# Weights split by casting and accumulating DMAs instead of by VectorE

## The chip, the cores and the metric

The kernel runs on one core of a Trainium2 chip, as one launch. The metric is device time in microseconds. A core has TensorE (PE, the matrix engine), VectorE (DVE), ScalarE (ACT), GpSimd (POOL) and SyncE (SP). Each engine works through its own queue strictly in order and waits on semaphores for the others. Transfers between DRAM and the on-chip memory are issued from an engine's queue: in the kernel before, nearly all from SP, and nine constants from POOL. They are carried by 16 shared DMA engines.

## The reference, cut to what matters

One inference step of a two-layer backbone on 640 tokens (512 latent, 128 context) of width 2048, all in float32:

```
layer 0: h = rmsnorm(x)*(1+scale)+shift          # scale, shift, gate: silu(c) @ mod_w[l] + mod_b[l]
         q,k,v,g_attn,hy_in,g_hy = split(h @ w_in)
         att = windowed attention (16 heads, per-head sink, rotary)
         hy  = order-2 long convolution of hy_in (FFT, implicit filters)
         x  += gate * (concat(att*silu(g_attn), hy*silu(g_hy)) @ w_out)
layer 1: h = rmsnorm(x)*(1+scale)+shift
         xb, gate = split(h @ c_w_in);  xc = depthwise_conv(xb)
         r, i = sigmoid(xc @ wa), sigmoid(xc @ wx)   # per head, two directions
         y  = linear recurrences over time in both directions
         x  += gate1 * ((y*silu(gate)) @ c_w_out)
outputs: rmsnorm(x), the new key and value cache, the final recurrent states
```

Nearly all the arithmetic is in five products of the 640 tokens with large weights: `w_in` (2048 x 6400), `w_out`, `c_w_in` (2048 x 4096), the gate matrices and `c_w_out`.

## The kernel before, in words

**Two-part products.** TensorE is given operands of type float32r, to which a value is rounded with fewer mantissa bits. To keep float32 precision each operand is split: a first part `h` (the value rounded to float32r) and a rest `l` (value minus first part). A product is the sum of three: first x first, first x rest, rest x first. For the weights these parts are the tiles `wh` and `wl`, for the tokens `h`/`l` (`mh`/`ml` or `md`, `xhl` in later stages).

**Halves.** Weights come as chunks of 128 output columns, each in two halves of 8 x 128 rows: one half is a tile of [128, 8, 128] float32, 512 KB. Each half is used by 48 matmuls (8 row blocks x 2 token halves x 3 products, lines 823 to 835), so that a half is the unit in which PE asks for weights. There are 241 of them.

**Stream (lines 453 to 519)** prepares halves in a fixed order. `load` issues the transfer of a half into a `raw` tile on the SP queue; `advance` makes `wh` by an ACT copy with a cast; `finish` makes `wl` by a DVE subtraction `raw - wh`, and then loads up to `RAWS` = 3 halves further. `keep_ahead`, called before each row block of a product, calls `advance` while fewer than two halves beyond the one in use are split; `take` hands a half to the product. The pool holds three tiles each of `raw`, `wh` and `wl`.

**Order.** The program is written out by a planner at build time: `Clock` estimates when each instruction would be done, `Order` is a heap of tasks (evictions, attention steps, filters, scans) that are let in between the matmuls when their estimated time has come. The engines then run their queues in exactly that order. `side_mods` (line 661) is one such task: it computes the later modulation vectors from `mod_w`, in tiles `macc` and `mprod`, and decides by the planner's estimate whether a piece goes to DVE alone or to ACT and POOL.

**Stages.** Start (norms, filter spectra, first modulations and the gate chunks), to 365 us of the profile; attention with the first chunks of `w_in`, to 690; the long convolution with the rest of `w_in`, to 1187; `w_out` with the first residual, to 1440; the recurrent layer (`c_w_in` and gate matrices), to 2050; `c_w_out` with the final norm, to the end. The weight stream runs through all of them without a break.

Of the kernel before, what the change touches and what calls it, by code (L numbers as in the profile page):

```python
# [10 lines left out]
F32 = mybir.dt.float32  # L11
F32R = mybir.dt.float32r
AF = mybir.ActivationFunctionType
ALU = mybir.AluOpType
# [7 lines left out]
GL = 644  # L22
P0 = 514
TWO_PI = 2.0 * np.pi
RAWS = 3
SPARE = 0.6


# [146 lines left out]
class Clock:  # L175
# [17 lines left out]
    def __init__(self):  # L193
        self.t = {"PE": 0.0, "V": 0.0, "S": 0.0, "G": 0.0, "Q": 0.0, "DMA": 0.0}
        self.table, self.last = None, 0.0
        self.writes, self.reads, self.start = {}, {}, {}
        self.held = {"V": [], "G": []}
# [255 lines left out]
class Stream:  # L453


    def __init__(self, engines, clock, pool, ahead=2):
        self.V, self.S, self.G, self.Q = engines
        self.pooled = False
        self.clock, self.pool, self.ahead = clock, pool, ahead
        self.src, self.raw, self.parts, self.left = [], {}, {}, {}  # L460
        self.loaded = self.split = self.taken = 0
# [4 lines left out]
    def load(self, n):  # L466
        while self.loaded < min(n, len(self.src)):
            i = self.loaded
            t = self.pool.tile([128, 8, 128], F32, tag="raw", name="raw")
            self.Q.dma_start(out=t, in_=self.src[i])  # L470
            self.raw[i] = t
            self.loaded += 1

    def advance(self):

        i = self.split
        if i >= len(self.src):
            return
        self.load(i + 1)
        raw = self.raw.pop(i)  # L480
        wh = self.pool.tile([128, 8, 128], F32R, tag="wh", name="wh")
        wl = self.pool.tile([128, 8, 128], F32R, tag="wl", name="wl")
        self.S.copy(wh, raw)
        self.parts[i] = (wh, wl)
        self.split += 1
        self.left[i] = raw
        Ring.order.spawn(self.rest(i))
# [6 lines left out]
    def finish(self, i):  # L494

        if i not in self.left:
            return
        raw, (wh, wl) = self.left.pop(i), self.parts[i]
        (self.G if self.pooled and i % 2 else self.V).tensor_sub(wl, raw, wh.bitcast(F32))
        self.load(i + 1 + RAWS)  # L500

    def take(self, od):
        i = self.taken
# [19 lines left out]
@with_exitstack  # L523
def tile_kernel(ctx: ExitStack, tc: tile.TileContext, A: dict, O: dict):
    with tc.manual_schedule():
        _kernel(ctx, tc, A, O)


def _kernel(ctx, tc, A, O):
# [4 lines left out]
    od = Ring.order = Order(clock)  # L534

    def pool_of(stack, name, bufs=1, **kw):
        return Pool(stack.enter_context(tc.tile_pool(name=name, bufs=bufs, **kw)), clock, bufs)
# [3 lines left out]
    wpool = pool_of(ctx, "wpool", bufs=3)  # L541
# [4 lines left out]
    r_acc = Bank(pacc, [128, 512], F32, "acc", 3)  # L546
    r_m = Ring(pmisc, [128, 512], F32, "m", 1)
    ws = Stream((V, S, G, Q), clock, wpool)
# [112 lines left out]
    def side_mods(groups, raws, accs, prods, ring):  # L661
        todo = [(l, g, k) for l, g in groups for k in range(16)]
        raw, n = {}, 0
        for j, (l, g, k) in enumerate(todo):
# [17 lines left out]
            for v in range(2):  # L682
                c, a = csil[:, k, v:v + 1], acc[v]
                while True:
                    if clock.t["V"] + IDLE[0] <= od.time and not left[v] and clock.ready([a], [a], "V") <= od.time:
                        if k == 0:
# [270 lines left out]
    with ExitStack() as st:  # L957
# [9 lines left out]
        msb = sp.tile([128, 512], F32, tag=f"ef{EF}", name="msb", bufs=1)  # L967
        csil32 = sp.tile([128, 16, 32], F32, tag=f"ef{EF + 1}", name="csil32", bufs=1)
# [16 lines left out]
        for i in range(2):  # L985
            G.dma_start(out=fil[i], in_=A["fil"][i])
        mods = Mods(
            [(0, 4 + g // 2 if g % 2 == 0 else g // 2) for g in range(8)],
            [(wpool, "raw", 3), (wpool, "wh", 3), (wpool, "wl", 3)], r_acc, csil32, msb,
        )  # L990
        AHEAD = 7
        mods.load(2)
# [627 lines left out]
            V.tensor_scalar(fr[:, :, i, :], yv[:, :, i, :], sc, None, op0=ALU.mult)  # L1620

    IDLE = [99]
    mods = ctx.enter_context(ExitStack())
    mp = pool_of(mods, "mods", bufs=1)
    r_raw = Ring(mp, [128, 512], F32, "mraw", 2)
# [261 lines left out]
    first_out = []  # L1887
    IDLE[0] = 0.5
    with ExitStack() as st:
# [332 lines left out]


    def out_project(op, layer, src, parts, first, keep, finish, xout, sqa, last=None):

        r_x = Ring(op, [128, T], F32, "xr", 3 if last else 2)
# [9 lines left out]
        def out(i, x, o):  # L2236
# [10 lines left out]
            def then():  # L2247
                r_x.free(x)
                if keep is not None:
                    Q.dma_start(out=keep[i], in_=o[:, 0:T])  # L2250
                if i == 0:
                    S.activation(sqa, o[:, 0:T], AF.Square)
                else:
                    while not r_sq.ready():
                        yield 0.3
                    sq = r_sq.get()
                    S.activation(sq, o[:, 0:T], AF.Square)
                    yield
                    V.tensor_add(sqa, sqa, sq)
                    r_sq.free(sq)  # L2260
                yield
                yield from finish(i, o)
                yield
                xout[i] = o
# [20 lines left out]
    first_lru = []  # L2285
    IDLE[0] = 0.3
    with ExitStack() as st:
# [38 lines left out]
    parts2, first_out, mixed_done = [None] * 16, [], {}  # L2326
    IDLE[0] = 99
    with ExitStack() as st:
# [447 lines left out]
```

## Time and profile before

| | us |
|---|---|
| median of 3 runs | 2297.33 (2296.53 to 2302.62) |
| profiled execution, its own time | 2299.91 |
| its span, first to last instruction | 2298.1 |
| PE busy | 2130.1 (93%) |
| DVE busy | 1673.0 (73%) |
| ACT busy | 1086.3 (47%) |
| POOL busy | 845.3 (37%) |

Busy time is the time in which an engine has an instruction running. An engine's idle time matters only where PE, directly or through others, waits for it. PE's matmuls overlap one another, so its busy time is an upper bound of its work. The granted TensorE clock is 0.976 of full speed over the span.

### The profile page before, as it was taken

To read this page: it belongs to the slowest core of one execution; us is meant where nothing else is said; L and a number is where in the kernel's file an instruction comes from. 1 tells how busy PE (TensorE), PEld (TensorE's weight loads), DVE (VectorE), ACT (ScalarE), POOL (GpSimd) and SP (SyncE) were. 2 spreads that over 40 slices of the span, in tenths; PEclk is the share of its full clock that TensorE was granted. 3 is DMA by queue.
4 is the path that set the end of the run, shared out by engine and by line. 5 is a ranking of instruction groups with operands and counts; after the bars stand their busy time and mean duration, and the time that the engine had idled before them with its cause. 6 is when DMAs were issued, how large, how long until landed. Compare 5 with 4: busy or idle time off the path is not lost. (4 is left out here: it accounts for less than half of the span.)

```text
span 2298.1 us, 37534 instructions
## 1 busy us (share of the span) xinstructions
PE 2130.1 (93%) x14567; PEld 2025.0 (88%) x14567; DVE 1673.0 (73%) x2560; ACT 1086.3 (47%) x1814; POOL 845.3 (37%) x678
## 2 busy tenths in 40 slices
PE   4899989988989999999998999899999999999997
PEld 1579888877878999999987999799999999999997
DVE  6968775898877888887887676787886667783334
ACT  5555555555553333333353333576565554662222
POOL 3424443445344666566563222444530101110002
PEclk9899999999999999999998999999999999999998
DMA  9864434222225444444455555333322222243223
GB/s 367 301 247 131 136 114 135 84 100 86 93 95 194 140 147 147 140 139 146 148 200 175 191 188 183 98 116 114 117 79 88 85 85 86 80 171 109 97 97 131
DMA packets 127449, 320.62 MB, mean 140 GB/s; under 512 B 14246, under 2 KB 22279, under 8 KB 127272
## 3 DMA queue, kind: packets, MB, share of 16 engines
q1 hardware_dynamic: 125480, 313.20, 40.5%
q0 software_dynamic: 1792, 5.04, 0.7%
q8 instruction: 114, 1.87, 0.3%
q14 instruction: 63, 0.52, 0.1%
HBM read 281.86 MB, written 36.32 MB: 138 GB/s over the span
## 5 line engine op out<-in xcount | busy, mean ns | idle before, releaser
L318 PE MATMUL acc<-h,wh 128*128 128x320 f32 x2544 | 810.0, 318 | 24.9 <-DVE xo L318 9.0
L318 PE MATMUL acc<-h,wl 128*128 128x320 f32 x2544 | 793.0, 312 | 0.0
L318 PE MATMUL acc<-l,wh 128*128 128x320 f32 x2544 | 792.4, 311 | 0.0
L318 POOL TENSOR_TENSOR macc<-macc,mprod 128x512 f32<-128x512 f32 x289 | 434.7, 1504 | 559.2 <-ACT mprod L318 474.1
L318 PEld LDWEIGHTS acc<-h,wh 128*128 128x128 f32 x2544 | 485.2, 191 | 36.0 <-DVE xo L318 9.3
L318 PEld LDWEIGHTS acc<-l,wh 128*128 128x128 f32 x2544 | 484.7, 191 | 0.1
L318 PEld LDWEIGHTS acc<-h,wl 128*128 128x128 f32 x2544 | 483.6, 190 | 0.0
L318 ACT CAST wh<-raw 128x1024 fp32r<-128x1024 f32 x241 | 252.4, 1047 | 413.0 <-PE acc L318 370.0
L318 DVE TENSOR_TENSOR wl<-raw,wh 128x1024 fp32r<-128x1024 f32 x241 | 318.0, 1320 | 171.5 <-ACT wh L318 169.2
L318 PE MATMUL acc<-mh,wh 128*128 128x320 f32 (+2 forms) x1024 | 318.9, 311 | 11.2 <-ACT mh L318 8.8
L318 ACT ACTIVATE mprod<-mraw,vec 128x512 f32<-128x512 f32 x289 | 209.1, 724 | 237.6 <-POOL macc L318 169.5
L318 PE MATMUL acc<-mh,wl 128*128 128x320 f32 (+2 forms) x1024 | 318.3, 311 | 0.0
L318 PE MATMUL acc<-ml,wh 128*128 128x320 f32 (+2 forms) x928 | 288.0, 310 | 2.4 <-DVE ml L318 2.4
L318 DVE SCALAR_TENSOR_TENSOR macc<-mraw,vec,macc 128x512 f32<-128x512 f32 x191 | 186.2, 991 | 100.8 <-DMA mraw<-in_mod_w_dram 77.3
L318 PEld LDWEIGHTS acc<-mh,wh 128*128 128x128 f32 x1024 | 193.2, 189 | 14.6 <-ACT mh L318 9.2
L318 PEld LDWEIGHTS acc<-mh,wl 128*128 128x128 f32 x1024 | 193.6, 189 | 0.0
L318 PEld LDWEIGHTS acc<-ml,wh 128*128 128x128 f32 x928 | 175.1, 189 | 4.1 <-DVE ml L318 3.7
L318 POOL COPY stout<-hs 128x1 f32<-128x1 f32 x32 | 20.5, 639 | 319.2 <-DVE hs L318 319.2
L318 PE MATMUL g<-xhl,wh 128*128 128x322 f32 x512 | 115.7, 314 | 2.2 <-ACT ri L318 2.2
L318 POOL TENSOR_TENSOR y<-y,t 128x256 f32<-128x256 f32 x80 | 84.2, 1072 | 43.0 <-DVE t L318 34.1
L318 POOL TENSOR_TENSOR xo<-xo,sq 128x384 f32<-128x384 f32 (+1 forms) x13 | 11.5, 916 | 239.8 <-ACT sq L318 239.8
L318 DVE SCALAR_TENSOR_TENSOR xo<-acc,modc,xr 128x128 f32<-128x128 f32 (+3 forms) x96 | 38.8, 434 | 82.6 <-PE acc L318 73.7
(303 smaller groups left out, 3369.4 us busy)
## 6 DMA issues: line engine op xcount, KB each, us to landing
mraw<-in_mod_w_dram SPq DMA_DIRECT2D x256, 256.0 KB, 3.3
raw<-in_w_in_dram SPq DMA_DIRECT2D x95, 512.0 KB, 4.0
mraw<-in_mod_w_dram SPq DMA_DIRECT2D x64, 512.0 KB, 7.4
raw<-in_c_in_dram SPq DMA_DIRECT2D x64, 512.0 KB, 3.7
raw<-in_c_out_dram SPq DMA_DIRECT2D x34, 512.0 KB, 3.9
raw<-in_w_out_dram SPq DMA_DIRECT2D x32, 512.0 KB, 4.0
hd<-ef SPq DMA_DIRECT2D x48, 256.0 KB, 3.9
raw<-in_c_gates_dram SPq DMA_DIRECT2D x16, 512.0 KB, 3.5
```

The lines of the kernel that those rows point to most:

```text
L318: f(*args, **kw)
```

## The change

From the attention stage on, halves take another way. `load` issues, on the POOL queue, a transfer from DRAM straight into `wh`, which casts to float32r on the way. `finish` makes `wl` in two steps: ACT writes minus `wh` into `wl`, and a second transfer from the POOL queue, from the same DRAM source, adds the weights to it. DVE has no part in it. The halves are then loaded up to index i + 1 when half i is finished. The pool holds two `raw`, four `wh` and three `wl` tiles (nine, as before). In the start stage halves go the old way, with `RAWS` = 2.

```diff
-RAWS = 3
+RAWS = 2
+WHS = 4
 class Stream:
-        self.pooled = False
+        self.adding = False
     def load(self, n):
         while self.loaded < min(n, len(self.src)):
             i = self.loaded
-            t = self.pool.tile([128, 8, 128], F32, tag="raw", name="raw")
-            self.Q.dma_start(out=t, in_=self.src[i])
+            if self.adding:
+                t = self.pool.tile([128, 8, 128], F32R, tag="wh", name="wh", bufs=WHS)
+                self.G.dma_start(out=t, in_=self.src[i])
+            else:
+                t = self.pool.tile([128, 8, 128], F32, tag="raw", name="raw", bufs=RAWS)
+                self.Q.dma_start(out=t, in_=self.src[i])
     def advance(self):
-        wh = self.pool.tile([128, 8, 128], F32R, tag="wh", name="wh")
+        wh = raw if raw.dtype == F32R else self.pool.tile([128, 8, 128], F32R, tag="wh", name="wh", bufs=WHS)
-        self.S.copy(wh, raw)
+        if wh is not raw:
+            self.S.copy(wh, raw)
     def finish(self, i):
         raw, (wh, wl) = self.left.pop(i), self.parts[i]
-        (self.G if self.pooled and i % 2 else self.V).tensor_sub(wl, raw, wh.bitcast(F32))
-        self.load(i + 1 + RAWS)
+        if wh is raw:
+            self.S.activation(wl, wh.bitcast(F32), AF.Identity, scale=-1.0)
+            self.G.dma_start(out=wl, in_=self.src[i], accum_op=ALU.add)
+        else:
+            self.V.tensor_sub(wl, raw, wh.bitcast(F32))
+        self.load(i + 2 if wh is raw else i + 1 + RAWS)
...
     IDLE = [99]
+    od.drain(lambda: not ws.raw)
+    ws.adding = True
```

Of the 241 halves, 21 keep the old way and 220 take the new one (74 of `w_in`, 32 of `w_out`, 80 of the recurrent layer, 34 of `c_w_out`). Since the planner decides again, the modulation pieces move too: `macc` additions on POOL go from 289 to 260, and those that DVE does alone from 190 to 219.

The first place is the last stage. Before, on DVE, with `wl` the rests, `acc` the sums of a product and `xo` its result:

```order
L318 TENSOR_TENSOR wl_21785<-raw_21620,wh_21784 128x1024
L318 SCALAR_TENSOR_TENSOR xo2_21721<-acc_21722,modc_77,xr_21719 128x320
L318 SCALAR_TENSOR_TENSOR xo2_21721<-acc_21745,modc_77,xr_21719 128x192
L318 SCALAR_TENSOR_TENSOR xo2_21721<-acc_21745,modc_77,xr_21719 128x128
L318 TENSOR_TENSOR wl_21843<-raw_21702,wh_21842 128x1024
L318 TENSOR_TENSOR sqa_21592<-sqa_21592,sq_21856 128x640
L318 TENSOR_TENSOR wl_21904<-raw_21740,wh_21903 128x1024
```

The subtractions leave DVE, and the evictions of the sums follow each other. What now stands on POOL at that place:

```order
L319 DMA wl_21354<-in_c_out_dram 128x1024
L319 DMA wh_21360<-in_c_out_dram 128x1024
L319 DMA wl_21438<-in_c_out_dram 128x1024
L319 DMA wh_21441<-in_c_out_dram 128x1024
L319 DMA wl_21499<-in_c_out_dram 128x1024
L319 DMA wh_21502<-in_c_out_dram 128x1024
```

Accumulating transfers (`wl`) and loads (`wh`) alternate. On ACT, at the same place:

```order
L319 ACTIVATE wl_21354<-wh_21283 128x1024
L319 ACTIVATE sqa_21342<-xo0_21350 128x640
L319 ACTIVATE xo0_21350<-xo0_21350,vec_74 128x640
L319 ACTIVATE wl_21438<-wh_21360 128x1024
L319 ACTIVATE sq_21482<-xo0_21350 128x640
L319 ACTIVATE xo0_21350<-xo0_21350,vec_74 128x640
L319 ACTIVATE wl_21499<-wh_21441 128x1024
```

Read with the rows of POOL: the accumulating transfer into `wl_21354` is followed by the load of `wh_21360`, which ACT negates into `wl_21438`, which the next accumulating transfer then writes.

The second place is POOL in the recurrent layer, where it collects the final states (`stout`) and sums the two directions (`hs`) of the scans. Before:

```order
L318 COPY stout_81<-hs_20834 128x1
L318 COPY stout_81<-hs_20848 128x1
L318 TENSOR_TENSOR hs_20834<-hs_20834,hs_20848 128x512
L318 TENSOR_TENSOR hs_20834<-hs_20834,hs_20848 128x128
L318 COPY stout_81<-hs_21027 128x1
L318 COPY stout_81<-hs_21047 128x1
```

And now, in the same stage:

```order
L319 DMA wl_20484<-in_c_gates_dram 128x1024
L319 DMA wh_20487<-in_c_in_dram 128x1024
L319 COPY stout_81<-hs_20530 128x1
L319 DMA wl_20568<-in_c_in_dram 128x1024
L319 DMA wh_20579<-in_c_in_dram 128x1024
L319 COPY stout_81<-hs_20550 128x1
L319 TENSOR_TENSOR hs_20530<-hs_20530,hs_20550 128x512
L319 TENSOR_TENSOR hs_20530<-hs_20530,hs_20550 128x128
L319 DMA wl_20665<-in_c_in_dram 128x1024
```

The weight transfers now stand in one queue with copies that wait for DVE's scans.

## Rows read from the trace of the kernel before

**Rows 1.** Windows by stage: length; each engine's busy us; clock; DMA share; GB/s.

```profile
393.00:690.00 297.00, 266.93 (x1978) 237.59 (x1980) 250.09 (x555) 163.01 (x380) 143.02 (x100) 0.99 0.29 93
690.00:1187.00 497.00, 476.27 (x3349) 465.86 (x3349) 404.31 (x509) 183.64 (x308) 301.79 (x243) 0.98 0.48 156
1187.00:1440.00 253.00, 234.71 (x1565) 227.66 (x1564) 177.43 (x217) 97.83 (x153) 74.34 (x47) 0.97 0.54 179
1440.00:2050.00 610.00, 584.14 (x3901) 578.49 (x3900) 460.62 (x643) 358.77 (x511) 159.23 (x130) 0.98 0.30 97
2050.00:2298.00 248.00, 232.91 (x1575) 231.05 (x1573) 94.35 (x155) 70.48 (x89) 11.51 (x13) 0.98 0.35 121
```

**Rows 2.** Chain of waits that ended last: share of the span by line.

```profile
PE acc L318 24%; PE g L318 4%; DVE w L318 1%; DVE xc L318 1%; DVE wl L318 1%; POOL macc L318 1%; DVE hs L318 1%; ACT mprod L318 0%; ACT ri L318 0%; DVE ri L318 0%; ACT wh L318 0%; ACT L318 0%; DVE xo L318 0%; DMA mixe<-gt 0%; DMA mraw<-in_mod_w_dram 0%
```

**Rows 3.** PE's waits in 690 to 1187 and 1440 to 2060: us, times, longest.

```profile
PE tz L318 <- DVE y L318: 12.4, 9, 2.6
PE tz L318 <- DVE zt L318: 2.4, 4, 1.3
PE tz L318 <- DVE ztp L318: 1.4, 1, 1.4
...
PE acc L318 <- DVE g L318: 7.3, 2, 6.2
PE acc L318 <- DVE lu L318: 5.6, 2, 2.8
```

**Rows 4.** The page's costliest groups: busy us, mean ns, idle before.

```profile
L318 ACT CAST wh<-raw 128x1024 fp32r<-128x1024 f32 x241 | 252.4, 1047 | 413.0 <-PE acc L318 370.0
L318 DVE TENSOR_TENSOR wl<-raw,wh 128x1024 fp32r<-128x1024 f32 x241 | 318.0, 1320 | 171.5 <-ACT wh L318 169.2
L318 DVE SCALAR_TENSOR_TENSOR macc<-mraw,vec,macc 128x512 f32<-128x512 f32 x191 | 186.2, 991 | 100.8 <-DMA mraw<-in_mod_w_dram 77.3
```

**Rows 5.** Tile raw: SP's issues, ns min/median/max, first to last us; times to landing.

```profile
L318 SPq DMA_DIRECT2D raw<-in_c_in_dram x64: 327/328/328, 1415.7 to 2013.8; - x64
L318 SPq DMA_DIRECT2D raw<-in_c_out_dram x34: 327/328/333, 2021.9 to 2254.9; - x34
L318 SPq DMA_DIRECT2D raw<-in_w_out_dram x32: 327/328/333, 1144.1 to 1408.6; - x32
L318 SPq DMA_DIRECT2D raw<-in_c_gates_dram x16: 327/328/328, 1465.8 to 1968.4; - x16
DMA to landing us min/median/max: 3.3/3.9/9.6
```

**Rows 6.** Groups on DVE in 393 to 690, then in 690 to 1187.

```profile
L318 DVE TENSOR_TENSOR wl<-raw,wh 128x1024 fp32r<-128x1024 f32 x21 | 27.3, 1300 | 3.3 <-ACT wh L318 3.1
...
L318 DVE TENSOR_TENSOR wl<-raw,wh 128x1024 fp32r<-128x1024 f32 x52 | 73.5, 1414 | 14.3 <-ACT wh L318 14.1
```

**Rows 7.** DMA issues from POOL: KB each, median us to landing.

```profile
band<-in_band_dram POOLq DMA_DIRECT2D x1, 192.0 KB, 3.4
```

**Rows 8.** Tiles psig, then invo (512 KB each): POOL's issues, times to landing.

```profile
L318 POOL DMA_DIRECT2D psig<-in_psig_dram x2: 538/542/547, 693.9 to 695.5; - x2
DMA to landing us min/median/max: 6.5/9.1/11.8
...
L318 POOL DMA_DIRECT2D invo<-in_invo_dram x2: 537/538/540, 694.4 to 696.0; - x2
DMA to landing us min/median/max: 8.5/10.7/12.9
```

**Rows 9.** Windows after these issues: columns as in rows 1.

```profile
694.00:698.00 4.00, 3.76 (x25) 3.76 (x26) 3.96 (x6) 1.20 (x4) 3.84 (x6) 1.00 0.96 303
698.00:702.00 4.00, 4.00 (x30) 4.00 (x29) 3.42 (x5) 1.05 (x1) 0.00 (x0) 1.00 1.07 350
702.00:706.00 4.00, 4.00 (x29) 4.00 (x29) 0.66 (x1) 0.84 (x2) 0.00 (x0) 1.00 1.11 386
```

**Rows 10.** The page's costliest groups: ACT's products for the modulation pieces.

```profile
L318 ACT ACTIVATE mprod<-mraw,vec 128x512 f32<-128x512 f32 x289 | 209.1, 724 | 237.6 <-POOL macc L318 169.5
```

**Rows 11.** POOL in time order: start, us, instruction, idle time before it.

```profile
374.92 1.29 POOL L318 TENSOR_TENSOR macc<-macc,mprod 128x512 f32<-128x512 f32 x1 [0.83 <-ACT mprod L318]
```

**Rows 12.** All waits: POOL for DVE's scans, us, times, longest.

```profile
POOL stout L318 <- DVE hs L318: 319.2, 31, 40.8
```

More of the change, by code (lines that the diff above doesn't have):

```diff
@@ L988, in _kernel @@
             [(0, 4 + g // 2 if g % 2 == 0 else g // 2) for g in range(8)],
-            [(wpool, "raw", 3), (wpool, "wh", 3), (wpool, "wl", 3)], r_acc, csil32, msb,
+            [(wpool, "raw", RAWS), (wpool, "wh", WHS), (wpool, "wl", 3)] * 2
+            + [(wpool, "wh", WHS), (wpool, "wl", 3), (wpool, "wh", WHS)], r_acc, csil32, msb,
         )
```

## The prediction

> **What bounds the kernel now.** I read the windows by stage first. From attention on PE is busy 267 of 297 us, 476 of 497, 235 of 253, 584 of 610 and 233 of 248 [rows 1]: in every stage PE is nearly full, and about 110 us of its 1905 us are idle. The chain of waits agrees: its largest entry is the matmuls of the projections, and the subtraction that makes `wl` has 1% [rows 2]. So DVE work that leaves is worth only the part of PE's idle time that DVE ends. PE's waits give this: in the long convolution 12.4 + 2.4 + 1.4 = 16.2 us, in the recurrent layer 7.3 + 5.6 = 12.9 us [rows 3]. What the change can gain is tens of microseconds; what it can lose depends on whether a half still arrives each time PE wants one.
>
> **How often PE wants a half.** The issues of the loads tell it, since each waits for a buffer that PE's progress frees. In `c_w_out` 34 loads start between 2021.9 and 2254.9: 233.0 / 33 = 7.06 us per half. In the recurrent layer 64 + 16 loads between 1415.7 and 2013.8: 598.1 / 79 = 7.57 us. In `w_out` 32 between 1144.1 and 1408.6: 264.5 / 31 = 8.53 us [rows 5]. In the long convolution 52 halves are split in 497 us, 9.56 us each, and in attention 21 in 297 us, 14.1 us each [rows 1, 6]; there PE has other work between halves. Before, three loads run ahead of the split; a load takes 3.9 us at the median [rows 5], and nothing of it shows on PE.
>
> **What the change removes.** 220 subtractions of 1.32 us, 290 us of DVE's time, and DVE's waits in front of them for ACT's cast (169.2 us for all 241) [rows 4]. Against it 29 more pieces of the modulation go to DVE, at 0.99 us some 29 us [rows 4]. ACT's work stays: 220 negations in place of 220 casts of 1.047 us. I take 1.05 us for one; from below it could not be shorter than the cast by much, from above it is twice a scaled 128x512 at 724 ns, 1.45 us [rows 4, 10]. POOL gets 440 issues at 0.54 us [rows 8], 238 us on an engine that is busy 11.5 us in the last stage and 302 of 497 in the long convolution [rows 1], less 29 additions. In the start stage one `raw` tile fewer costs nothing as long as a load lands within the two halves before its use, 14 us against 3.9 us; if that cover failed, at most 21 halves could each lose part of a landing time.
>
> **What it adds: a loop.** `finish(i)` puts the accumulating transfer of half i on POOL's queue and right behind it the load of half i + 1, and no other load is out. That half is negated by ACT only when it has landed, and the next accumulating transfer waits on POOL for the negation, with the next load behind it. So the weight stream has a period of its own, whatever PE does:
>
> - issue of the accumulating transfer, 0.54 us [rows 8];
> - landing of the load behind it. A casting load of 192 KB took 3.4 us from its issue [rows 7]. Call d the time of 512 KB on the wire. While the constants of the convolution were loaded all queues together moved 350 and 386 GB/s [rows 9], so d = 524 KB / 370 = 1.4 us undisturbed. A load of 512 KB alone then lands after 3.4 + (320/512) d = 4.3 us, near the 3.9 us that SP's loads take. But it queues: from issues 0.5 us apart, psig landed at 693.9 + 6.5 = 700.4, the 512 KB of invo at 694.4 + 8.5 = 702.9, the second pair at 707.3 and 708.9 [rows 8], one after the other, 2.5 and 1.6 us for the second of a pair. So the load lands later by the data time of the accumulating transfer, m d, less the 0.54 us of its head start;
> - the negation, 1.05 us, and two handovers. POOL starts 0.83 us after it went idle behind a 0.724 us product of ACT [rows 10, 11], so a handover is about 0.1 us.
>
> The sum is P = 0.54 + 3.4 + 0.625 d + m d - 0.54 + 1.05 + 0.2 = 4.65 + (m + 0.625) d.
>
> No transfer of before accumulates, so m must be bounded. From below: the added transfer runs beside the load, not ahead of it, and the loop is 0.54 + 4.3 + 1.25 = 6.1 us. If it costs what a copy costs, m = 1, P is 6.93 us. From above: d = 2.5 us, the longer step of invo's rows, and m = 2 give 11.2 us. I take m = 2, since the transfer has to fetch both the weights from DRAM and what lies in `wl`, and d = 1.4 us, because in the two last stages the DMA engines are busy only 30% and 35% [rows 1]: P = 8.33 us.
>
> The Trainium skill says the same of such transfers ("Collectives: The Full Stack", section "The bandwidth ceiling: the fold count and why AG ≠ RS ≠ AR"): an add in the transfer path reads two sources through one ring, and moves about half of what a copy moves. No run here has shown it. By that rule the sum is the one with m = 2; were it wrong, the one with m = 1.
>
> POOL's issue is short in the trace even next to a full DVE: both invo issues took 0.54 us [rows 8] in windows where DVE was busy 3.96 of 4 us [rows 9]. The Trainium skill warns of the opposite ("SBUF — State Buffer", section "Who interferes with whom"): some DVE instructions lock GpSimd out, and with it the writing of its DMA descriptors. By the rows an issue costs 0.54 us; by the rule one could wait for a DVE instruction, about 1 us more in each of two issues of a loop, and P would be 10.3. The trace does not agree at this one place; I keep 0.54.
>
> **The sum.** `c_w_out`: 33 (8.33 - 7.06) = +42 us. Recurrent layer: 79 (8.33 - 7.57) = +60 us. `w_out`: 8.33 is under 8.53, 0. Long convolution and attention: 0, the loop is hidden by PE's 9.56 and 14.1 us. DVE's relief: 16.2 us of waits in the long convolution can go, I take 10; in the later stages the loop replaces them. Together +92 us on the profiled execution's 2299.9, so 2392; that execution lies 2.6 us above the median of the runs, which makes 2389 us. The end of the kernel moves with PE, whose new wait is for the accumulating transfer into `wl`. What is late next is ACT: the instructions queued behind a negation that waits for its load, `sq` and evictions among them, are late too, but PE is then waiting for the same loop.
>
> **Rivals.**
>
> *The loop fits, and DVE's relief shows.* If the added transfer runs beside the load or costs a copy's time, P is 6.1 to 6.93 us, under every stage's 7.06. Then PE's waits on DVE of rows 3 go, 12.4 + 7.3 + 5.6 = 25 us: 2272 us. For it speaks that POOL is nearly idle at the end and the DMA engines have room; against it the in-order landings of rows 8, and a margin of 0.13 us.
>
> *The accumulating transfer is slow, or other traffic slows both.* The convolution's and `w_out`'s DMA shares are 48% and 54% [rows 1]. With d = 2.0 us, between the rows' 1.4 and 2.5, P is 9.9 us: 33 x 2.84 + 79 x 2.33 + 31 x 1.37 + 52 x 0.34 = 94 + 184 + 42 + 18 = +338 us, 2635 us. With d = 2.5 us it is 11.2: 137 + 287 + 83 + 85 = +592, 2889 us.
>
> *POOL's queue holds the weights up.* In the recurrent layer the 32 copies into `stout` wait for DVE's scans, now with weight transfers behind them in the same queue. POOL stood 319.2 us in 31 such waits, up to 40.8 us [rows 12]. Before, nothing hung on it. If a tenth of it lands on a loop that is already at PE's pace (8.33 against 7.57) it adds 32 us: 2421 us. It decides from where the scans come later than the planner put them; I count it with the forecast's own range.
>
> *The gain and the loss cancel.* At P = 7.4 us the last stage loses 33 x 0.34 = 11 us and the others nothing, about the 10 us of relief: 2298 us.
>
> **How the numbers follow.** Forecast (P from 7.8 to 9.2, that is 24 + 18 - 10 = +32 to 71 + 129 + 21 - 10 = +211; 2330 to 2508): 0.48. Slow transfer: 0.22. Loop fits: 0.23. Cancel: 0.05. The remaining 0.02 is that something else, as ACT held at a negation, costs a little. The likeliest case gives 2389 us. The range from 2262 to 2660 takes in the fitting loop and the milder half of the slow one, and leaves about a tenth at each end. A measurement of this kernel tells about 0.3% (7 us) from no change: faster 0.23, within it 0.05, slower 0.72.
>
> **What would show it.** In the profile after: PE's largest new wait is for DMA into `wl`; in the last stage accumulating transfers are issued every 8 to 9 us and not every 7.06, with ACT's negations waiting for the load of `wh`; PE's busy share there falls below 90%, while attention keeps its length. The landing time of `wl`'s transfers gives m: about 6 us where it is 2, under 5 where it is 1. The forecast is wrong if `wh` lands within 4.5 us behind an accumulating transfer, since then m is near 0 and PE stays full; or if attention and the long convolution, where I have 0, carry most of the change.

## The result, and the profile after

The change makes the kernel slower: 2585.31 us at the median of 4 runs (2575.27 to 2589.75), against 2296.93 us before on the same chip, a ratio of 1.1244 with an interval of 1.1203 to 1.1285. That is +288 us where +92 was forecast; the time lies in the range from 2262 to 2660. The profiled execution has a span of 2579.9 us, 281.8 more than before.

The windows of the kernel after, cut at its own stages (columns as in rows 1: length; busy us of PE, PEld, DVE, ACT and POOL; granted clock, DMA share, GB/s):

```profile
393.00:719.00 326.00, 289.57 (x2070) 257.85 (x2069) 238.30 (x540) 162.15 (x378) 162.24 (x144) 0.97 0.49 129
719.00:1238.00 519.00, 475.91 (x3270) 463.20 (x3269) 343.76 (x477) 154.35 (x264) 280.90 (x308) 0.96 0.70 188
1238.00:1550.00 312.00, 254.31 (x1557) 241.98 (x1556) 123.42 (x194) 78.28 (x126) 73.37 (x85) 0.90 0.73 199
1550.00:2266.00 716.00, 619.99 (x3909) 606.94 (x3908) 404.86 (x562) 378.55 (x544) 297.14 (x323) 0.92 0.60 146
2266.00:2580.00 314.00, 249.84 (x1563) 240.14 (x1561) 58.06 (x126) 73.19 (x93) 58.42 (x78) 0.93 0.62 158
```

Beside [rows 1]: DVE has its relief (404 to 344 us in the convolution, 94 to 58 in the last stage), and PE is worse off: busy 80% of the last stage, 94% before. Where the time came in is read from the starts of PE's matmuls of three kinds; of each the row gives the count, the duration in ns (min/median/max) and the first and last start:

```profile
L319 PE MATMUL sc<-kl,qhl x80: 276/338/628, 418.1 to 691.3; 128*128 128x384 f32 x32, 128*128 128x512 f32 x32, 128*128 128x256 f32 x16
L319 PE MATMUL acc<-mh,wh x1024: 275/309/636, 1238.5 to 2563.7; 128*128 128x320 f32 x160, 128*128 128x384 f32 x6, 128*128 128x256 f32 x5
L319 PE MATMUL g<-xhl,wh x512: 304/312/637, 1614.8 to 2220.6; 128*128 128x322 f32 x171
```

The same rows of before:

```profile
L318 PE MATMUL sc<-kl,qhl x80: 276/338/522, 412.7 to 676.5; 128*128 128x384 f32 x32, 128*128 128x512 f32 x32, 128*128 128x256 f32 x16
L318 PE MATMUL acc<-mh,wh x1024: 274/309/632, 1190.5 to 2281.6; 128*128 128x320 f32 x160, 128*128 128x384 f32 x6, 128*128 128x256 f32 x5
L318 PE MATMUL g<-xhl,wh x512: 304/311/473, 1504.5 to 2010.6; 128*128 128x322 f32 x171
```

The last start of `sc`, the first of `mh`, and the first and last of `g` cut each span into five parts: up to the end of attention, the long convolution, `w_out` with the recurrent layer's start, the recurrent layer, and the rest with `c_out`. Before they are 676.5, 514.0, 314.0, 506.1 and 287.5 us long. Each part holds the same matmuls in all these profiles, to within some twenty. What each profile has more or less than that:

| us | attention | convolution | w_out | recurrent | rest | sum |
|---|---|---|---|---|---|---|
| the change | +15 | +33 | +62 | +100 | +72 | +282 |
| e1_three_ahead | +14 | +32 | +62 | +103 | +71 | +282 |
| e2_no_add | +5 | -9 | +22 | +16 | +21 | +54 |
| e3_old_way | +1 | +6 | -10 | 0 | +3 | 0 |
| e4_dma_cast | +2 | 0 | -4 | -2 | +2 | -2 |
| e5_three_loads | +12 | +5 | 0 | -4 | +6 | +19 |
| e6_to_conv | +17 | +36 | -12 | 0 | +3 | +44 |
| e7_load_first | +12 | +28 | -7 | -14 | +8 | +26 |
| e8_little_traffic | +19 | +20 | +46 | +90 | +73 | +248 |
| e9_from_w_out | +2 | +8 | -8 | -4 | +10 | +7 |
| e10_load_first_late | -1 | +3 | -4 | 0 | +10 | +9 |

e3, which runs like before, shows how far a single part can be off: up to 10 us, partly given back in the next one.

The loop stands in the chain of waits of the last stage, in order of time (start, us, what):

```profile
2383.66 6.49 DMA wh<-in_c_out_dram
2390.15 0.02 issue
2390.18 0.04 ACTq L319
2390.21 0.04 issue
2390.26 1.07 ACT wl L319
2391.33 0.29 issue
2391.62 0.43 POOL wl L319
2392.05 0.13 issue
2392.18 6.24 DMA wh<-in_c_out_dram
```

From one load's issue to the next is 8.52 us, and the next round, to the load at 2400.45, takes 8.27: load, negation, accumulating transfer, load. PE is nowhere in this chain. On the page the same is seen from ACT, which now waits for loads before its negations:

```profile
L319 ACT ACTIVATE wl<-wh 128x1024 fp32r<-128x1024 f32 x220 | 233.2, 1060 | 839.6 <-DMA wh<-in_c_out_dram 206.7
L319 POOL DMA_DIRECT2D wl<-in_c_out_dram x34 | 30.0, 883 | 251.7 <-ACT wl L319 233.8
...
wh<-in_c_out_dram POOLq DMA_DIRECT2D x34, 512.0 KB, 6.5
wl<-in_c_out_dram POOLq DMA_DIRECT2D x34, 512.0 KB, 5.6
```

Before, the cast in this place waited for PE (370.0 of 413.0 us [rows 4]): the weights were early. Now they are late.

### The profile page after: what moved, and what is told of

The parts are those of the page before. It is cut to its first block, busy times and chain, and to the rows that moved or that the text cites. A ratio compares the mean times of both kernels' runs of the same rounds, so it can differ in the third digit from the quotient of the medians.

```text
span 2579.9 us, 37346 instructions
## 1 busy us (share of the span) xinstructions
PE 2225.7 (86%) x14567; PEld 2095.1 (81%) x14567; DVE 1447.7 (56%) x2378; ACT 1056.4 (41%) x1776; POOL 1026.8 (40%) x1089
## 3 DMA queue, kind: packets, MB, share of 16 engines
q0 software_dynamic: 65152, 235.75, 39.5%
## 5 line engine op out<-in xcount | busy, mean ns | idle before, releaser
L319 ACT ACTIVATE wl<-wh 128x1024 fp32r<-128x1024 f32 x220 | 233.2, 1060 | 839.6 <-DMA wh<-in_c_out_dram 206.7
L319 POOL TENSOR_TENSOR macc<-macc,mprod 128x512 f32<-128x512 f32 x260 | 388.0, 1492 | 146.2 <-ACT mprod L319 135.2
L319 PE MATMUL acc<-mh,wl 128*128 128x320 f32 (+2 forms) x1024 | 332.4, 325 | 47.7 <-DMA wl<-in_c_out_dram 36.2
L319 DVE SCALAR_TENSOR_TENSOR macc<-mraw,vec,macc 128x512 f32<-128x512 f32 x220 | 207.3, 964 | 212.8 <-POOL macc L319 131.0
L319 PE MATMUL acc<-ml,wh 128*128 128x320 f32 (+2 forms) x960 | 309.9, 323 | 6.2 <-DVE ml L319 6.1
L319 ACT ACTIVATE mprod<-mraw,vec 128x512 f32<-128x512 f32 x260 | 186.8, 718 | 189.9 <-POOL macc L319 169.4
L319 POOL DMA_DIRECT2D wl<-in_c_in_dram x64 | 57.2, 893 | 280.8 <-ACT wl L319 264.5
L319 POOL DMA_DIRECT2D wl<-in_w_in_dram x74 | 66.0, 892 | 256.9 <-ACT wl L319 238.9
L319 PEld LDWEIGHTS g<-xhl,wh 128*128 128x128 f32 x512 | 98.5, 217 | 40.8 <-ACT ri L319 36.2
L319 POOL DMA_DIRECT2D wl<-in_c_out_dram x34 | 30.0, 883 | 251.7 <-ACT wl L319 233.8
L319 POOL DMA_DIRECT2D wl<-in_w_out_dram x32 | 28.5, 889 | 231.9 <-ACT wl L319 223.6
```

Of the source, the lines that this page charges most:

```text
L319: f(*args, **kw)
```

## The experiments

My theory: the loop with one load out sets the pace, and of its length the accumulating transfer's data is a part. The rivals: the doubled traffic, the new buffers, POOL's queue, or other traffic that slows the loop.

**e2_no_add**: the second transfer only copies, so `wl` is the weight itself and not the remainder.

```
-            self.G.dma_start(out=wl, in_=self.src[i], accum_op=ALU.add)
+            self.G.dma_start(out=wl, in_=self.src[i])
```

> The second transfer copies with a cast and does not add (wl is then the weight, so the outputs are other ones). All else is the changed kernel. It measures m, the data time of an accumulating transfer in copies. Loop theory with m = 2 and 1.4 us per copy: the loop is 1.4 us shorter, 7.0 in place of 8.4 us in the quiet last stage, landing of wh behind it 5.1 us in place of 6.5; 2585 falls to 2350 to 2420 us. Rival, an add costs what a copy costs (m = 1): within 1% of 2585 us and the landing stays at 6.5 us.

Measured: 2355.41 us (2350.18 to 2359.11), ratio 1.0229 [1.0206, 1.0251]. The chain of this kernel in its last stage, in order of time:

```profile
2191.59 4.94 DMA wh<-in_c_out_dram
2196.53 0.02 issue
2196.55 0.04 ACTq L319
2196.58 0.04 issue
2196.63 1.07 ACT wl L319
2197.70 0.28 issue
2197.98 0.43 POOL wl L319
2198.41 0.10 issue
2198.51 4.85 DMA wh<-in_c_out_dram
```

The round takes 6.92 us; the prediction's sum for a transfer at a copy's cost was 6.93. The round with the add is 1.6 us longer than this one, about one more d of 1.4: so m is about 2. The page's DMA issues say it again (512 KB each, median us to landing, of this kernel):

```profile
wh<-in_c_out_dram POOLq DMA_DIRECT2D x34, 512.0 KB, 5.1
wl<-in_c_out_dram POOLq DMA_DIRECT2D x34, 512.0 KB, 4.3
```

But the kernel is still 2.3% slower, although 6.92 us is less than PE's 7.06. The rival of the prediction by which such a loop fits (2272 us) would have been wrong even with m = 1: a loop that just keeps PE's pace in a quiet round has no slack for the rounds that take longer, and `w_out`, the recurrent layer and the rest lose 16 to 22 us each.

**e3_old_way**: only the buffers of the change (two `raw`, four `wh`, the rotation at the start); `adding` is never set.

```
     od.drain(lambda: not ws.raw)
-    ws.adding = True
```

> Only the buffers of the change (two raw, four wh tiles, and the order of tiles for the first modulations); every half goes the old way through SP, ACT and DVE. Loop theory: 2297 us within 10, the whole loss is in the new way. Rival, the shorter run-ahead of two raw loads costs by itself: over 2320 us.

Measured: 2298.42 us (2293.95 to 2312.86), ratio 0.999 [0.9971, 1.0008]. The buffers cost nothing.

**e4_dma_cast**: the casting load on POOL stays, SP loads the same half once more into `raw`, and DVE subtracts as before. No negation, no add, and as many bytes.

```
+                self.full[i] = self.pool.tile([128, 8, 128], F32, tag="raw", name="raw", bufs=RAWS)
+                self.Q.dma_start(out=self.full[i], in_=self.src[i])
...
-            self.S.activation(wl, wh.bitcast(F32), AF.Identity, scale=-1.0)
-            self.G.dma_start(out=wl, in_=self.src[i], accum_op=ALU.add)
+            self.V.tensor_sub(wl, self.full.pop(i), wh.bitcast(F32))
```

> wh comes by the casting load on POOL's queue, the same half once more as raw on SP's queue, and DVE subtracts: no negation, no accumulating transfer; two loads of 512 KB per half as in the change. Loop theory: POOL's queue waits for nothing but free tiles, the loads run on, no loop, 2280 to 2310 us, the last stage at 7.1 us per half. Rival 1b, twice the weight traffic is the cost by itself (load on the DMA engines): above 2400 us.

Measured: 2294.84 us (2292.08 to 2304.44), ratio 0.9975 [0.9962, 0.9989]: 0.25% under the kernel before, the lowest ratio of all. Its windows for `w_out`, the recurrent layer and `c_out`:

```profile
1190.00:1440.00 250.00, 231.75 (x1559) 225.95 (x1558) 171.61 (x209) 78.16 (x137) 109.32 (x94) 0.96 0.76 254
1440.00:2050.00 610.00, 590.56 (x3948) 585.78 (x3947) 462.02 (x643) 283.73 (x431) 203.29 (x213) 0.99 0.52 167
2050.00:2298.00 248.00, 229.76 (x1548) 227.09 (x1546) 91.32 (x153) 38.03 (x56) 27.95 (x44) 0.97 0.57 186
```

The DMA engines carry as much as after the change (436 and 437 MB in all), and no stage is longer than before by more than 2 us. Twice the traffic is no cause by itself; nor are the casting load and POOL's 220 issues for it.

**e1_three_ahead** was to have three loads out, with `raw` tiles as further buffers for `wh`.

```
-                t = self.pool.tile([128, 8, 128], F32R, tag="wh", name="wh", bufs=WHS)
+                tag, n = ("raw", RAWS) if i % 3 == 2 else ("wh", WHS)
+                t = self.pool.tile([128, 8, 128], F32R, tag=tag, name="wh", bufs=n)
...
-        self.load(i + 2 if wh is raw else i + 1 + RAWS)
+        self.load((i + 4 if i >= 30 else i + 2) if wh is raw else i + 1 + RAWS)
```

> The change with two more wh tiles (the two raw tiles, idle after the start stage) and loads up to three halves beyond the finished one, in place of one. Loop theory (the cost is that only one load is out, behind an accumulating transfer and in front of a negation): the loop is gone, PE no longer waits for wl, the last stage is back at about 7.1 us per half, 2300 us within 25. Rival 1, the transfers themselves are the limit (the add is slow in the queue): nothing changes much, above 2520 us. Rival 2, POOL and ACT stand in line for the weights whatever is loaded: between, 2350 to 2450 us, with the loss in attention and the long convolution left (48 us in the changed kernel).

Measured: 2594.24 us (2582.8 to 2600.31), ratio 1.1262 [1.1228, 1.1296]. My edit reused the name `n`, which in this loop bounds how many halves are loaded, so that it never ran further ahead: one load was out as before. The run says nothing of three loads. It repeats the change on another chip with two more tiles for `wh`, and they alone give nothing back.

**e5_three_loads** is e1 with a name of its own for the number of tiles.

```
-                tag, n = ("raw", RAWS) if i % 3 == 2 else ("wh", WHS)
+                tag, bufs = ("raw", RAWS) if i % 3 == 2 else ("wh", WHS)
```

> What e1 was meant to be: in e1 a name was used twice (the number of tiles overwrote the number of halves to load), so that still only one load was out, and its 2594 us only repeat the changed kernel. Here the two further tiles do hold loads: three are out beyond the finished half. Loop theory (one load out, behind an accumulating transfer and in front of a negation; period 8.4 us quiet, about 9 us busy): the loop is gone, last stage at 7.1 us per half, 2300 us within 25. Rival 1, the add itself is the limit (the queue needs 2.9 + 1.4 us of data per half and more beside other traffic): above 2450 us. Rival 2, POOL and ACT stand in line for the weights whatever is loaded: 2350 to 2450 us, PE's waits on DVE g and ACT ri in the recurrent layer stay (43 and 32 us in the changed kernel).

Measured: 2319.05 us (2308.57 to 2321.53), ratio 1.0058 [1.004, 1.0076]. The negations now wait for PE to free their tile, not for a load (page of this kernel; then its window in the last stage):

```profile
L319 ACT ACTIVATE wl<-wh 128x1024 fp32r<-128x1024 f32 x220 | 233.1, 1060 | 440.0 <-PE acc L319 426.4
```

```profile
2060.00:2310.00 250.00, 239.46 (x1596) 235.41 (x1594) 57.15 (x122) 73.79 (x93) 56.44 (x75) 0.99 0.76 190
```

With the same matmuls, the same transfers and the same bytes (six modulation pieces went to another engine), 16 us are left of the change's 288: 2319.05 against 2303.14 us before on the same chip. In `c_out` the accumulating transfers are 7.06 us apart at the median, PE's own pace; PE is full again, and its granted clock in the last stage is 0.99 where it was 0.93. The loss was the single load in the loop.

**e7_load_first** breaks the loop at another place: the next load is issued ahead of the accumulating transfer.

```
             self.S.activation(wl, wh.bitcast(F32), AF.Identity, scale=-1.0)
+            self.load(i + 2)
             self.G.dma_start(out=wl, in_=self.src[i], accum_op=ALU.add)
```

> Four wh tiles as in the change; only the order of two issues on POOL is turned: the next load goes ahead of the accumulating transfer, so that it waits neither for the negation nor behind the add. Loop theory: two halves per turn of the loop, about 9.3 us for two, no limit to PE's 7.06: 2300 us within 25. Rival 1, the add's data time in the queue: above 2450 us. Rival 2, standing in line: 2350 to 2450 us.

Measured: 2325.71 us (2320.74 to 2330.78), ratio 1.0096 [1.0076, 1.0115]. On the same chip the kernel before takes 2303.14, so 23 of the 288 us are left: one place in POOL's queue is worth 266 us. In attention and the convolution this kernel is 40 us behind, not much less than the change (48); in the three parts after these it is 13 us ahead of before. Why the convolution stays 28 us longer is open: between 688 and 1230 us PE stands still for 40 us, before for 21 between 690 and 1190, and it waits for `wl` only 1.4 us of them.

**e6_to_conv**: the new way ends with the long convolution.

```
     first_lru = []
+    ws.adding = False
```

> The new way only to the end of the long convolution; from w_out on the old way with two raw tiles. Loop theory with the stages adding up: the 48 us that attention and the long convolution are longer in the changed kernel, and nothing behind them: 2345 us within 10. Rival, the loss is made up behind (PE's later waits shrink, or the modulation pieces move): under 2325 us.

Measured: 2346.1 us (2339.28 to 2355.21), ratio 1.0186 [1.0161, 1.0211]. That is 43 us over the kernel before on the same chip, 2303.14, where 48 were expected. In the profile the first two parts are 53 us longer and the others 9 us shorter together, as much as a part is off in e3. So the stages add up, as far as a single profile can tell.

**e8_little_traffic**: most of the modulation weights' bytes are left out.

```
...
-                    Q.dma_start(out=raw[n], in_=A["mod_w"][l2, g2, k2 // 2][:, k2 % 2])
+                    w, c = A["mod_w"][l2, g2, k2 // 2][:, k2 % 2], 512 if n < 2 else 64
+                    Q.engine.dma_start(out=raw[n][:, 0:c], in_=w[:, 0:c])
+                    clock.note("Q", "dma_start", (), dict(out=raw[n], in_=w))
```

> The change, with the order of every engine left as it is, but from the third piece on each load of modulation weights brings 64 of 512 columns and the arithmetic runs over what the tile holds; so 254 x 224 KB = 57 MB of traffic are left out of attention, the long convolution and w_out, and the outputs differ. Theory that other traffic lengthens the loop there: the median interval between accumulating transfers falls from 9.7 to about 9 us in the convolution and from 10.0 to 8.9 in w_out, wh lands there in 6.5 instead of 7.2 us; 30 halves x 1.1 and half of the convolution's 33 us come back, 2585 - 50 = 2535 us, 2515 to 2555. Rival, the order of the work on ACT and POOL holds the loop back in these stages, not the traffic: intervals stay at 9.7 and 10.0 us, 2585 us within 10. The recurrent layer and c_out, which load no modulation weights, keep 8.9 us by both.

Measured: 2534.05 us (2523.37 to 2548.42), ratio 1.1021 [1.0987, 1.1055]. The total is where the traffic theory put it, its steps are smaller, so that the total owes something to luck: the median interval between accumulating transfers falls from 9.7 to 9.5 us in the convolution and from 10.0 to 9.4 in `w_out`, the two parts give back 29 us together in the profile, and the recurrent layer, which was to stay, has 10 us less. The landing of `wh` does what the theory says. The 32 loads of `w_out`, last line of tile `wh` on POOL, first of the kernel after, then of this run:

```profile
DMA to landing us min/median/max: 6.3/7.6/10.6
```

```profile
DMA to landing us min/median/max: 6.3/7.0/9.6
```

At the mean that is 7.80 and 7.23 us, 0.57 less, and the mean round is shorter by about as much, 9.65 us where it was 10.12. Not all other traffic is gone: from an accumulating issue to the landing of the load behind it the other queues still move 416 KB on average in `w_out`, where they moved 757. So other traffic lengthens the loop there, and less of it gives back 16 of the 62 us.

**e9_from_w_out** and **e10_load_first_late**: e5 and e7 with the old way in attention and the convolution, the two candidates for a faster kernel.

```
-    ws.adding = True
...
     first_lru = []
+    ws.adding = True
```

> Attention and the long convolution with the old way, from w_out on the new way with three loads out (the raw tiles hold weights too, and half i + 4 is loaded when i is finished). Theory that the single load in the loop is all of the loss, and that DVE was not on the path: the time of before, the start as in the kernel before and from w_out on as in the run with three loads, 1190 + 1110 = 2300 us, ratio 0.998 to 1.003. Rival, POOL's 238 us of issues or the doubled traffic cost something by themselves: 1.005 or more. Rival, DVE's relief of some 170 us from w_out on shows at last, its 13 us of waits in the recurrent layer go: 0.994 or less.

> Attention and the long convolution with the old way, from w_out on the new way with the next load issued ahead of the accumulating transfer (as in the run with the load first). That run was behind in the convolution (its first matmul of w_out at 1230 us, 1190 before) but needed 1094 us from there, 1108 before. If that was DVE's relief, the start of before and the rest of that run give 1190 + 1094 = 2285 us, ratio 0.992 to 0.996. Rival: it had only moved work that the longer convolution had covered (modulation pieces done earlier), or a single profile's scatter; then 2300 us as the run with three loads from w_out on, 0.998 to 1.003.

Measured: e9 2301.82 us (2298.37 to 2307.2), ratio 1.0004 [0.9994, 1.0013]; e10 2306.94 us (2297.66 to 2311.64), ratio 1.0024 [1.0012, 1.0035]. e10's rival was right: what e7 had won after the convolution was work that the longer convolution had covered, or scatter. e9's windows for the three last stages:

```profile
1190.00:1440.00 250.00, 235.00 (x1564) 229.29 (x1564) 132.61 (x199) 84.50 (x132) 77.19 (x83) 0.97 0.86 237
1440.00:2050.00 610.00, 593.77 (x3967) 589.09 (x3966) 373.85 (x568) 364.07 (x523) 258.43 (x299) 0.99 0.71 169
2050.00:2300.00 250.00, 235.54 (x1559) 231.68 (x1557) 55.50 (x121) 70.73 (x89) 55.63 (x74) 0.97 0.76 185
```

DVE has 45 + 87 + 39 = 171 us less to do there than before [rows 1], and the time is the same. With the loop out of the way, the relief the change was made of is worth nothing here: PE was full.

## Why the prediction was right in direction and too small

**The mechanism was right.** One load is out, and load, negation and accumulating transfer follow each other. Term by term, forecast against the round above: issue 0.54, measured 0.56; landing of the load 3.4 + 0.625 d + 2 d - 0.54 = 6.54 with d = 1.4, measured 6.49; negation 1.05, measured 1.07; handovers 0.2, measured 0.10 + 0.29. Sum 8.33, measured 8.52 and 8.27 in the next round. m = 2 was right (e2). The rule that the prediction names beside it is one on collectives; that it holds for a transfer within one core, e2 alone shows.

**The step that failed is the size of P**: "d = 1.4 us, because in the two last stages the DMA engines are busy only 30% and 35%", so 8.33 us, used for all stages alike. These shares are those of before; after the change they are 60% and 62%, and 73% in `w_out`. The 8.33 us are the period of a quiet round. Measured it is 10.1 us at the mean in `w_out`, where a load takes 7.80 us to land and not 6.54, and 8.9 in the two last stages. With it fell two terms of the sum: "`w_out`: 8.33 is under 8.53, 0. Long convolution and attention: 0".

| us | forecast | measured |
|---|---|---|
| attention and convolution, with DVE's relief | -10 | +48 |
| w_out | 0 | +62 |
| recurrent layer | +60 | +100 |
| c_out and rest | +42 | +72 |

The part called `w_out` holds 38 halves, 6 of them of the recurrent layer.

Two errors lie in it, and they are of different size. First, a stage's mean hides where PE is dense. Between the starts of ACT's casts in the trace of before, 18 of 31 intervals in `w_out` are under 7.3 us and 20 of 52 in the convolution under 8.3; the mean of 8.53 or 9.56 us is made by a few long ones. To price this I replayed those 217 starts: each half comes P after the one before it at the earliest, two are in hand, PE takes each when it wants it or when it comes. With P = 8.33 the five parts lose 2, 0, 13, 54 and 49 us, 118 in all (an estimate): 13 us for `w_out` instead of 0, and the forecast's two other terms much as they stood. This error is small.

Second, and larger, P itself. The trace of the kernel after gives each term of a round from the starts and the landing of its records (us, mean of the 32, 80 and 34 rounds):

| us | forecast | w_out | recurrent | c_out |
|---|---|---|---|---|
| accumulating issue to load's issue | 0.54 | 0.59 | 0.60 | 0.56 |
| landing of the load | 6.54 | 7.80 | 6.74 | 6.76 |
| negation | 1.05 | 1.06 | 1.06 | 1.06 |
| two handovers, with any wait there | 0.2 | 0.67 | 0.54 | 0.52 |
| P | 8.33 | 10.12 | 8.94 | 8.90 |

With the three measured P, and 8.33 in the first two parts, the replay gives 2, 0, 60, 105 and 70 us, 238 of the 282. In the convolution the mean interval of 10.4 us holds PE's own pauses too; with it that part would lose 22 us, an upper bound. So 11 of its 33 us at the least, and 13 of attention's 15, are not the loop's by this estimate.

In `w_out` the landing is most of what was missed, 1.26 of 1.79 us. It grows with what other queues move meanwhile: they move 757 KB per round there, against some 200 in the two last stages, and a line through the 32 rounds gives 1.0 us for each 512 KB, from 6.3 us at none (correlation 0.86). e8 took part of that traffic away, and the landing fell. The handovers are the smaller share there; in the two last stages they are the larger, 0.3 of the 0.6 us against 0.2 for the landing. The prediction counted no wait in them, for ACT's other work or for POOL. In `w_out` 29 of the 32 negations start within 0.15 us of their load's landing, and the three late ones make 0.25 us of the mean.

**DVE's relief** in the convolution, -10 us, did not show. In e5, where the loop is gone and DVE has its relief, that part is 5 us longer than before: PE's waits for `y`, `zt` and `ztp` fall from 16.2 to 11.3 us, but 8.8 us of waits for DVE's `yhl` are new. Only e2 is shorter there, by 9 us, no more than a part can be off. From `w_out` on, e9's 171 us less on DVE give 1.0004.

**The rivals.** The loop that fits: refuted by e2 twice, in m and in the belief that 6.93 us would do. Slow transfer or other traffic: its number, 2635, is nearer than the forecast's, and it had `w_out` right, in P (9.9) and in the reason; but d was not 2.0 in the two last stages, which carry 172 of the 282 us at 8.9 (their landing of 6.75 us makes d 1.5). A POOL issue that waits for a DVE instruction, P = 10.3: the issues are 0.56 to 0.60 us apart in the table above, and 0.63 in the convolution, where DVE is busy 66% of the time; this is not what made `w_out`'s 10.1. Such a wait does exist, and is short: of e2's 440 issues for weights 13 take over 0.65 us, at most 0.83 in place of 0.54, and all 13 run beside a TENSOR_SCALAR on DVE, as only 46 of the 440 do. In the prediction's rows the first of the two issues had none beside it, and beside the second it was the TENSOR_SCALAR that took long (128x8 in 1.88 us). `stout` in POOL's queue did not decide: in the recurrent layer an accumulating transfer is issued 0.35 us after its negation's end at the mean, 0.30 at the median. POOL's wait for the scans shrank from 319.2 us [rows 12] to this (all waits of the kernel after):

```profile
POOL stout L319 <- DVE hs L319: 17.4, 10, 3.5
```

**The signs to look for.** Accumulating issues every 8 to 9 us in the last stage: 8.5 at the median. Landing of about 6 us for m = 2: 5.6. PE under 90% there: 80%. Attention keeps its length: it did not, +15, of which the replay explains 2; with three loads out e5 has +12, and without the new way e9 has +2. This remainder belongs to the new way and not to its loop; what it is stays open. PE's largest new wait was to be for the transfer into `wl`: it is, with 36.2 + 11.4 + 4.9 + 4.4 = 56.9 us over the four weight sources. The longest single lines are these; in the recurrent layer PE is mostly seen waiting for the gates, although there too the negations start at their load's landing, 0.08 us after it at the median:

```profile
PE acc L319 <- DVE g L319: 42.8, 7, 7.5
PE acc L319 <- DMA wl<-in_c_out_dram: 36.2, 25, 4.0
PE g L319 <- ACT ri L319: 31.9, 13, 4.5
```

## What to carry to other kernels

When a change puts a load behind work that itself waits for an earlier load, count how many loads are out: with one, the latency of every step adds up to a period, and the remedy here was a further load in flight (e5) or one line moved ahead in the queue (e7). Such a period must be well below the densest demand and not just below a stage's mean. Price it in the busiest stage, not in the quiet one: there the same load lands later behind other queues' data, 7.80 us here instead of 6.5, and the loop pays this in every round. And work taken off an engine that the full engine seldom waits for is worth what those waits are, here nothing.

## What the runs showed of the hardware

An accumulating transfer of 512 KB from DRAM into SBUF costs more than the copy in each respect measured here. Its data takes about one copy's time more (1.6 us in a round), it lands in 5.6 instead of 4.3 us, and its issue on POOL takes longer. The issues of tile `wl` in `c_out`, ns min/median/max, of the kernel after and then of e2:

```profile
L319 POOL DMA_DIRECT2D wl<-in_c_out_dram x34: 878/884/902, 2263.1 to 2555.8; - x34
```

```profile
L319 POOL DMA_DIRECT2D wl<-in_c_out_dram x34: 537/537/570, 2077.2 to 2328.7; - x34
```

The load issued right behind it takes as long, 877 ns at the median in `c_out` and 537 in e2. The next issue began 0.56 us after it all the same, so the loop hardly felt this. The share of the DMA engines' time, for the same 65152 packets and 235.75 MB on the same queue, first of the kernel after, then of e2:

```profile
q0 software_dynamic: 65152, 235.75, 39.5%
```

```profile
q0 software_dynamic: 65152, 235.75, 32.5%
```

Of spans of 2579.9 and 2352.5 us these are 1019 and 765 us, a third more. Traffic of other queues delays such a chain of two transfers: by 1.0 us for each 512 KB in `w_out`. And TensorE's clock followed the loop: in the stages where PE paused in each round the mean granted clock was 0.90 to 0.93, a mixture of its levels of 2.4 and 1.2 GHz, and with the loop broken 0.99 in the last stage (e5). This is not where the time went: PE's busy time is 96 us longer than before for as many matmuls (2225.7 and 2130.1 us), but no term of the round is PE's, so that where the loop sets the pace a slower PE waits less and ends no later.
